# Attention outputs stored in one piece, transfers moved to GpSimd's queue, and a new filling plan in a hybrid decoder block

## The chip, the cores and the metric

The kernel runs on one core of a Trainium2 chip. The metric is the device time of one execution in microseconds (us); the time of a kernel is the median of its runs.

## The reference, cut to what matters

One layer of a decoder: RMSNorm, native sparse attention (three branches with gates), residual, RMSNorm, SwiGLU feed-forward, residual, final RMSNorm. 512 tokens, width 2048, 16 heads of 128 in 4 groups, feed-forward width 5632, all in float32.

```python
h = x
h = h + nsa_mixer(rmsnorm(h, g1), ...)       # DEPTH = 1: layer 0 is the attention mixer
h = h + swiglu(rmsnorm(h, g2), w_in, w_out)
return rmsnorm(h, g3)

# nsa_mixer: proj = h @ w_in gives q, three pairs of k and v, and gates
p_c = masked_softmax(q @ kcc + bias, mask)   # 31 compressed blocks
o_c = p_c @ vcc
...                                          # o_s: selected blocks; o_w: sliding window
o = gates[0] * o_c + gates[1] * o_s + gates[2] * o_w
return o.reshape(S, 2048) @ w_out
```

With 512 tokens there are 8 selectable blocks and up to 16 may be chosen, so the selected branch sees every earlier token, as the window does.

## The kernel before, in words

**Precision.** Each float32 operand is split into a high and a low part (ScalarE, ACT, copies the high part; VectorE, DVE, subtracts). A product is three matmuls (`three`, lines 267 to 269): high x high, low x high, high x low. Weights come as granules of up to 128 x 1024 through the class `Weights`: `load` issues the DMA (line 81) on the queue that `W.queue` names, `split` makes `whi` and `wlo` (lines 97, 98), `take` hands out the next granule and first lets the splits run three granules ahead and the loads three more. There are three raw and four converted buffers.

**The attention stage** (lines 630 to 899) does two kinds of work on TensorE (PE). The first is attention itself, head by head, with the 512 queries in four blocks of 128 (`t`, or `kt` for keys):
- `scores(h, t)`: matmuls into the PSUM tile `s`, DVE adds the bias and takes the maximum (line 791), ACT takes the exponential into `P[t]` (line 793), one part for each branch; the compressed branch goes to `CX[t]`.
- `finish(h, t)`: DVE multiplies by gate over sum (line 805), transposes in blocks of 32 (line 806), and SyncE's queue (SP) stores `P[t]` to memory as `d_p` in four DMAs (line 808).
- `fetch(t)`: SP loads it back, turned, into `PT` (tile `ptr`, line 812).
- `turn(h, b, kt)`: ACT and DVE split a part of `PT` into `pth` and `ptl` (lines 829, 831, 833). `b` is the branch, -1 the compressed one.
- `values(h, b, kt)`: PE multiplies with the values into the PSUM tile `o` (`three`, or line 844 for the compressed branch).
- `head_out(h)`: for heads 0 to 11 the output `o` is split into high and low (`of0`, `of1`; lines 292, 293) and stored in `d_o` (line 855); heads 12 to 15 go straight into `hn_h` and `hn_l`, whose old content is no longer needed by then.

The four `P` are views of two tiles: blocks 0 and 2 share one, 1 and 3 the other.

The second kind of work fills PE in between: `dense()`, a generator that makes the projections of later heads (`qpair`, `kpair`, `vpair`; 32 steps of 650 nominal ns each) and at last four `partial(cb)` (24 steps each), the output projection of heads 0 to 11 for 1024 of the 2048 columns. During the last `qpair` the outputs of heads 0 to 11 come back from memory into `hn_h`, `hn_l` (`reload_o`, line 696). A `partial` loads 512 KB of `x` into the one staging tile (line 702), DVE adds the product (line 717), and the sum goes to `d_h` (line 718).

**Order.** Each engine and each queue works in the order in which its instructions are written out. The program fixes this order by hand: each head has 12 steps, in which the turns, values, fetches of this head stand beside the scores and finishes of the next. After each step `pump(h, step)` draws steps from `dense()` until their nominal sum reaches a goal: 20800 per head up to 13 heads, 18300 after that, always four steps of a head ahead of the position. `drain_to` draws what must be there. Through the stage `W.queue` is GpSimd's queue (POOL); all other DMAs of the stage but one are on SP's.

Of the kernel before, what the change touches and what calls it, by code (L numbers as in the profile page):

```python
# [10 lines left out]
F32 = mybir.dt.float32  # L11
F32R = mybir.dt.float32r
I32 = mybir.dt.int32
AF = mybir.ActivationFunctionType
OP = mybir.AluOpType
# [4 lines left out]
S, D, H, DH, G, HPG = 512, 2048, 16, 128, 4, 4  # L20
NT, KC = S // 128, D // 128
# [152 lines left out]
def nsa_block(ctx: ExitStack, tc: tile.TileContext, x, rel_bias, mix_g, ffn_g, fin_g, w_in, w_out,  # L174
              pos_k, w1k, w2k, pos_v, w1v, w2v, f_in, f_out, onehot, out):
    nc = tc.nc
    mm, act, dve, pool = nc.tensor.matmul, nc.scalar.activation, nc.vector, nc.gpsimd
# [6 lines left out]
    dram = ctx.enter_context(tc.tile_pool(name="dram", bufs=1, space=DRAM))  # L184
# [10 lines left out]
    hn_h, hn_l = hn_t = [hnp.tile([128, KC, S], F32R, name=f"hn_{x}") for x in "hl"]  # L195
    d_t = dram.tile([H, UL], F32, name="d_t")
    d_u = dram.tile([128, H * UL], F32, name="d_u")
    d_c = dram.tile([H, 16 * CL], F32, name="d_c")
    d_o = dram.tile([12, 2, 128, S], F32, name="d_o")
    d_h = dram.tile([S, 256 * N_SPILL], F32, name="d_h")  # L200
    d_r = dram.tile([NT, 128, D], F32, name="d_r")
    d_a = dram.tile([NF // 2, 128, 2 * S], F32, name="d_a")
# [87 lines left out]
    def split_from(psum_ap, hi, lo, scale=None):  # L290
        if scale is None:
            act(hi, psum_ap, AF.Copy)
            dve.tensor_tensor(lo, psum_ap, hi.bitcast(F32), op=OP.subtract)
        else:
            act(hi, psum_ap, AF.Copy, scale=scale)
            dve.scalar_tensor_tensor(lo, psum_ap, scale, hi.bitcast(F32), op0=OP.mult, op1=OP.subtract)
# [53 lines left out]
    with ExitStack() as st1:  # L350
# [11 lines left out]
        with ExitStack() as st0:  # L362
# [79 lines left out]
            p = bank([128, 512])  # L442
            for i in range(N_WARM):
                nc.tensor.transpose(p[:, 128 * (i % 4):128 * (i % 4 + 1)], ident, ident)
            p = bank([128, KC])
# [10 lines left out]
            for q in range(4):  # L456
# [22 lines left out]
                if q == 3:  # L479
                    p = bank([128, S])  # L480
# [100 lines left out]
        for i in range(8):  # L581
# [10 lines left out]
            if i == 1:  # L592
                p = ps1.tile([128, 128], F32, name="tr")
# [27 lines left out]
        p = ps1.tile([96, G, 128], F32, name="tr")  # L621
# [8 lines left out]
    with ExitStack() as st2:  # L630
        ap_ = st2.enter_context(tc.tile_pool(name="ap", bufs=2))
        ps2 = st2.enter_context(tc.tile_pool(name="ps2", bufs=2, space=PSUM))
        kv_tiles(ap_, 1, bufs=1)
        runs = [32 * (2 * t + 3) for t in range(NT)]
        two = [ap_.tile([128, 4 * runs[t]], F32, name=f"p{t}", bufs=1) for t in (2, 3)]
        P = [two[t % 2][:, :4 * runs[t]].rearrange("p (j r) -> p j r", j=4) for t in range(NT)]
        CX = [ap_.tile([128, 32], F32, name=f"cx{t}", bufs=1) for t in range(NT)]
        PT = ap_.tile([128, 4, PT_STEP * 3 + runs[3]], F32, name="ptr", bufs=1)
        d_p = [dram.tile([4, 32, 4, runs[t]], F32, name=f"d_p{t}") for t in range(NT)]
        for t in range(2):  # L640
            pool.memset(two[t], 0.0)
        for t in range(NT):
            pool.memset(CX[t], 0.0)
        done = {"n": 0, "ns": 0}

        def stage_tile():
            return ap_.tile([128, 1024], F32, name="stage", bufs=1)
# [7 lines left out]
        def qpair(h0):  # L655
            ps = proj2()
            end = q_out(ps, h0)
            for i in range(4):
                yield from ws(ps, i, W.take(), end=end)
                if h0 == H - 2 and i < 3:  # L660
                    reload_o(i)
            done["n"] += 1
            yield None

# [27 lines left out]
            yield None  # L692

        def reload_o(i):
            for part, t in enumerate((hn_h, hn_l)):
                nc.sync.dma_start(t[:, 4 * i:4 * i + 4].bitcast(F32),
                                  d_o[4 * i:4 * i + 4, part].rearrange("h p s -> p h s"))

        def partial(cb):
            st = stage_tile().rearrange("p (t c) -> p t c", t=NT)  # L700
            c = slice(256 * cb, 256 * (cb + 1))
            nc.sync.dma_start(st, x[:, c].rearrange("(t p) c -> p t c", p=128))
            ps = [p.rearrange("p (t c) -> p t c", t=2) for p in proj2()]
            for i in range(3):
                w = W.take()
                for t in range(NT):
                    if i == 2 and t == 2:
                        W.ahead(3)
                    for k in range(4):
                        h = 4 * i + k  # L710
                        three(ps[t // 2][:, t % 2], hn_h[:, h, tok(t)], hn_l[:, h, tok(t)], w[0][:, k], w[1][:, k],
                              h == 0 and t % 2 == 0, h == 11)
                        if k % 2:
                            yield 650
                    if i == 2 and t % 2:
                        b = t // 2
                        dve.tensor_tensor(st[:, 2 * b:2 * b + 2], st[:, 2 * b:2 * b + 2], ps[b], op=OP.add)
            nc.sync.dma_start(d_h[:, c].rearrange("(t p) c -> p t c", p=128), st)
            done["n"] += 1
            yield None  # L720

# [12 lines left out]
        STEPS = 12  # L734

        def pump(h, step):
            at = h + (step + 4) / STEPS
            goal = 20800 * min(at, 13) + 18300 * max(at - 13, 0)
            while done["ns"] < goal:
                c = next(stream, "end")  # L740
                if c == "end":
                    return
                done["ns"] += c or 0
# [66 lines left out]
        def fetch(t):  # L810

            nc.sync.dma_start(PT[:, :, PT_STEP * t:PT_STEP * t + runs[t]], d_p[t].rearrange("j a i r -> (j a) i r"))
# [6 lines left out]
        def turn(h, b, kt):  # L819
            n = S - 128 * kt  # L820
            th = ap_.tile([128, 512], F32R, name="pth", bufs=3)
            tl = ap_.tile([128, 512], F32R, name="ptl")
            rows = 128 if b >= 0 else 96
            if b < 0:
                src = arrived(rows, 64, 0, PT_STEP + 64)
            else:
                src = arrived(rows, PT_STEP * kt + 32 * (kt + 1) * b + 32 * kt, kt, PT_STEP + 32 * b)
            th4, tl4 = (x[:rows, :n].rearrange("p (t i s) -> p t i s", i=4, s=32) for x in (th, tl))
            act(th4, src, AF.Copy)
            if b < 0:  # L830
                dve.tensor_tensor(th4[32:64], src[32:64], th4[32:64].bitcast(F32), op=OP.subtract)
            else:
                dve.tensor_tensor(tl4, src, th4.bitcast(F32), op=OP.subtract)
            HS[h]["t", b, kt] = th[:rows, :n], tl[:rows, :n]

        def values(h, b, kt):
            s, g = HS[h], h // HPG
            first = "o" not in s
            if first:
                s["o"] = ps2.tile([128, 512], F32, name="o", bufs=1)  # L840
            th, tl = s.pop(("t", b, kt))
            o = s["o"][:, 128 * kt:]
            if b < 0:
                mm(o, vcc[:, g], th, start=first, stop=True, skip_group_check=True)
            else:
                vh, vl = (v[:, kt, 128 * b:128 * (b + 1)] for v in VV[g % 2])
                three(o, vh, vl, th, tl, first, False)

        def head_out(h):
            o = HS[h]["o"]  # L850
            if h < 12:
                f = [ap_.tile([128, S], F32R, name=f"of{i}", bufs=1) for i in range(2)]
                split_from(o, *f)
                for i in range(2):
                    nc.sync.dma_start(d_o[h, i], f[i].bitcast(F32))
            else:
                split_from(o, hn_h[:, h], hn_l[:, h])
            del HS[h]
# [2 lines left out]
        load_bias(0)  # L861
        load_bias(1)
        for i in range(4):
            scores(0, 3 - i)
            if i:
                finish(0, 4 - i)
            if i > 1:
                fetch(5 - i)
            pump(-1, min(9 + i, 11.7))
        for h in range(H):  # L870
            seq = [(b, kt) for kt in (3, 2, 1, 0) for b in (0, 1)] + [(-1, 0)]
            for i in range(STEPS):
                if i == 4:
                    load_bias(h + 2)
                if i in (0, 3):
                    fetch(1 - i // 3)
                if i < 9:
                    turn(h, *seq[i])
                if i == 8 and h + 1 < H:
                    fetch(3)  # L880
                    fetch(2)
                if i == 0:
                    finish(h, 0)
                if h + 1 < H:
                    if i == 2:
                        drain_to(needed(h + 1))
                    if i % 3 == 2:
                        scores(h + 1, 3 - i // 3)
                    elif i % 3 == 0 and i:
                        finish(h + 1, 4 - i // 3)  # L890
                if 2 <= i < 11:
                    if i == 2 and h % HPG == 0:
                        drain_to(h)
                    values(h, *seq[i - 2])
                    if i == 10:
                        head_out(h)
                pump(h, i)
        W.queue = nc.sync
# [591 lines left out]
```

## Time and profile before

| | |
|---|---|
| median of 3 runs | 2137.48 us (2137.11 to 2138.2) |
| profiled execution | 2137.68 us, its span 2136.0 us |
| PE, weight load, DVE, ACT, POOL busy | 98%, 91%, 77%, 43%, 6% |
| mean granted clock of TensorE | 0.996 |
| read from memory, written | 323.67 MB, 73.50 MB |
| attention stage | about 200 to 710 us of the span |

Busy shares are of the span. A PE that is shown busy need not be at its peak, since matmuls are pipelined and their ends are modelled. An engine that idles off the critical path costs nothing by that. In lists of waits the columns are: engine and tile that waited, line, what ended the wait, then microseconds in total, number of times, and the longest.

### The profile page before, as it was taken

Reading aid. Unit: us, or ns where it says so; the run is one execution under the profiler, and the core shown is the slowest. Engines: PE = TensorE matmul, PEld = TensorE weight load, DVE = VectorE, ACT = ScalarE, POOL = GpSimd, SP = SyncE. Lnnn points to the kernel's source line nnn. Section 1 sums busy time; section 2 is a strip of 40 time slices with the busy share of each in tenths; the row PEclk is TensorE's granted clock in tenths of the full one; section 3 lists DMA queues with packets and bytes.
Section 4 is the critical chain, followed back from the end, with each engine's and each line's share of the span. In section 5 each row is a group of like instructions: output and inputs, shape, how many; then the busy total and the mean of one; then the engine's idle time right before and its main releaser. Section 6 shows DMA issues by size and latency. Waiting matters only on the chain.

```text
span 2136.0 us, 37198 instructions
## 1 busy us (share of the span) xinstructions
PE 2103.2 (98%) x14697; PEld 1949.5 (91%) x14697; DVE 1634.8 (77%) x2680; ACT 922.9 (43%) x1433; POOL 118.2 (6%) x195
## 2 busy tenths in 40 slices
PE   9999999999998999999999999999999999999998
PEld 7898788898988889899999999999999888999996
DVE  5565777878776357898888888888888787877785
ACT  5344454555544234444444343443434444544344
POOL 1000111111100000000000000000000000001000
PEclk9999999999999999999999999999999999999999
DMA  7555777776787643344434344433344776878894
GB/s 226 174 158 149 195 203 202 194 209 197 207 295 211 218 137 111 118 130 128 129 126 122 122 126 129 129 119 125 123 129 129 256 278 220 299 268 308 307 336 143
DMA packets 279147, 394.37 MB, mean 185 GB/s; under 512 B 34763, under 2 KB 208891, under 8 KB 278332
## 3 DMA queue, kind: packets, MB, share of 16 engines
q1 hardware_dynamic: 255324, 289.68, 43.5%
q0 software_dynamic: 21744, 98.12, 13.3%
q10 hardware_dynamic: 1904, 4.20, 0.5%
q8 instruction: 115, 1.88, 0.4%
q14 instruction: 60, 0.49, 0.1%
HBM read 323.67 MB, written 73.50 MB: 186 GB/s over the span
## 4 chain that ended last, share of the span: by engine, by line
PE 87%; DVE 5%; DMA 4%; ACT 2%; issue 2%; SPq 1%; POOL 0%; ACTq 0%; DVEq 0%; POOLq 0%
PE f L268 19%; PE f L269 19%; PE f L267 19%; PE proj L267 7%; PE proj L268 6%; PE proj L269 6%; DMA d_p<-p 1%; DVE wlo L98 1%; DMA ptr<-d_p 1%; PE pp L269 1%; PE pp L268 1%; PE pp L267 1%; PE po L269 1%; PE po L267 1%; PE po L268 1%
## 5 line engine op out<-in xcount | busy, mean ns | idle before, releaser
L98 DVE TENSOR_TENSOR wlo<-raw,whi 128x1024 fp32r<-128x1024 f32 (+1 forms) x226 | 270.6, 1200 | 117.2 <-ACT whi L97 116.7
L97 ACT ACTIVATE whi<-raw 128x1024 fp32r<-128x1024 f32 (+1 forms) x226 | 234.4, 1040 | 230.4 <-DVE raw L989 124.7
L989 DVE TENSOR_TENSOR tlo<-tt,thi 128x1536 fp32r<-128x1536 f32 (+2 forms) x135 | 197.1, 1460 | 110.1 <-ACT thi L1091 89.1
L267 PE MATMUL f<-hn_h,whi 128*128 128x256 f32 x984 | 271.7, 276 | 0.8 <-ACT E L1049 0.8
L269 PE MATMUL f<-hn_h,wlo 128*128 128x256 f32 x984 | 271.6, 276 | 0.0
L268 PE MATMUL f<-hn_l,whi 128*128 128x256 f32 x984 | 271.6, 276 | 0.0
L1086 ACT ACTIVATE whi<-raw 128x1024 fp32r<-128x1024 f32 x123 | 126.1, 1057 | 292.2 <-DVE raw L989 281.9
L267 PE MATMUL proj<-hn_h,whi 128*128 128x512 f32 x512 | 204.1, 399 | 0.5 <-ACT hn_h L402 0.5
L268 PE MATMUL proj<-hn_l,whi 128*128 128x512 f32 x512 | 200.7, 392 | 0.3 <-DVE hn_l L403 0.3
L269 PE MATMUL proj<-hn_h,wlo 128*128 128x512 f32 x512 | 200.9, 392 | 0.0
L267 PEld LDWEIGHTS f<-hn_h,whi 128*128 128x128 f32 x984 | 184.7, 188 | 1.2 <-ACT E L1049 1.2
L269 PEld LDWEIGHTS f<-hn_h,wlo 128*128 128x128 f32 x984 | 184.7, 188 | 0.0
L268 PEld LDWEIGHTS f<-hn_l,whi 128*128 128x128 f32 x984 | 184.7, 188 | 0.0
L1091 ACT ACTIVATE thi<-tt 128x1536 fp32r<-128x1536 f32 x82 | 121.8, 1486 | 84.8 <-PE f L268 75.3
L989 DVE TENSOR_TENSOR wlo<-raw,whi 128x1024 fp32r<-128x1024 f32 x123 | 147.0, 1223 | 0.0
L267 PE MATMUL proj<-whi,hn_h 128*128 128x256 f32 (+2 forms) x496 | 146.7, 296 | 0.0
L269 PE MATMUL proj<-whi,hn_l 128*128 128x256 f32 (+2 forms) x496 | 146.0, 294 | 0.0
L268 PE MATMUL proj<-wlo,hn_h 128*128 128x256 f32 (+2 forms) x496 | 145.9, 294 | 0.0
L269 PE MATMUL f<-whi,tlo 128*128 128x512 f32 x320 | 124.9, 390 | 0.6 <-DVE tlo L989 0.6
L268 PE MATMUL f<-wlo,thi 128*128 128x512 f32 x320 | 125.0, 391 | 0.0
L267 PE MATMUL f<-whi,thi 128*128 128x512 f32 x320 | 124.7, 390 | 0.0
L269 PEld LDWEIGHTS proj<-hn_h,wlo 128*128 128x128 f32 x512 | 96.5, 189 | 21.5 <-DVE wlo L98 0.2
(323 smaller groups left out, 6087.1 us busy)
## 6 DMA issues: line engine op xcount, KB each, us to landing
raw<-in_ffn_w_in SPq DMA_DIRECT2D x135, 512.0 KB, 3.8
raw<-in_ffn_w_out SPq DMA_DIRECT2D x88, 512.0 KB, 5.7
rawx<-in_ffn_w_in SPq DMA_DIRECT2D x41, 512.0 KB, 4.8
rawx<-d_a SPq DMA_DIRECT2D x31, 512.0 KB, 5.2
ah<-d_s POOLq DMA_DIRECT2D x16, 896.0 KB, 7.0
al<-d_s POOLq DMA_DIRECT2D x16, 896.0 KB, 9.5
raw<-in_nsa_w_in SPq DMA_DIRECT2D x24, 512.0 KB, 5.1
raw<-in_nsa_w_in POOLq DMA_DIRECT2D x24, 512.0 KB, 4.7
```

Source lines behind the costliest of these rows:

```text
L97: self.nc.scalar.activation(hi[:, :n], src, AF.Copy)
L98: self.nc.vector.tensor_tensor(lo[:, :n], src, hi[:, :n].bitcast(F32), op=OP.subtract)
L267: mm(o, ah, bh, start=start, stop=False, skip_group_check=True)
L268: mm(o, ah, bl, start=False, stop=False, skip_group_check=True)
L269: mm(o, al, bh, start=False, stop=stop, skip_group_check=True)
L989: dve.tensor_tensor(o, a, b, op=OP.subtract)
L1086: act(h, r, AF.Copy)
L1091: act(h, ttf, AF.Copy)
```

## The change

- `d_o` becomes three arrays of four heads in float32. `head_out` copies `o` once (ACT) into the staging tile and stores that, 12 stores of 256 KB instead of 24.
- `reload_o(i)` loads four heads in one DMA into `hn_l`, on GpSimd's queue instead of SP's; a new `split_o(k)` then splits two heads in place. It stands twice in the last `qpair` and four times in the first `partial`.
- A `partial`'s load of `x` and store of `d_h` go to GpSimd's queue; the load is written out at the second granule instead of at the start.
- Each of the four `P` has a tile of its own, all set to zero, block 3 first. `of0` and `of1` are gone. The compressed branch takes no `ptl` tile.
- `pump`: the lead over the position is 4 + max(5 - 2 x position, 0) steps, 11 at one head before the first, 4 from position 2.5 on. After 13 heads the goal grows by 22500 per head instead of 18300. Ahead of head 0, filling is drawn before each block of scores instead of after, and a fetch is issued ahead of the finish of its turn of the loop.
- `values` of the compressed branch and `head_out` move from step 10 to step 11.

```diff
-    d_o = dram.tile([12, 2, 128, S], F32, name="d_o")
+    d_o = [dram.tile([4, 128, S], F32, name=f"d_o{i}") for i in range(3)]
...
-        two = [ap_.tile([128, 4 * runs[t]], F32, name=f"p{t}", bufs=1) for t in (2, 3)]
-        P = [two[t % 2][:, :4 * runs[t]].rearrange("p (j r) -> p j r", j=4) for t in range(NT)]
+        P = [ap_.tile([128, 4, runs[t]], F32, name=f"p{t}", bufs=1) for t in range(NT)]
...
-        for t in range(2):
-            pool.memset(two[t], 0.0)
-        for t in range(NT):
+        for t in reversed(range(NT)):
             pool.memset(CX[t], 0.0)
+            pool.memset(P[t], 0.0)
...
                 if h0 == H - 2 and i < 3:
                     reload_o(i)
+                if h0 == H - 2 and i > 1:
+                    split_o(i - 2)
...
         def reload_o(i):
-            for part, t in enumerate((hn_h, hn_l)):
-                nc.sync.dma_start(t[:, 4 * i:4 * i + 4].bitcast(F32),
-                                  d_o[4 * i:4 * i + 4, part].rearrange("h p s -> p h s"))
+            pool.dma_start(hn_l[:, 4 * i:4 * i + 4].bitcast(F32), d_o[i].rearrange("h p s -> p h s"))
+
+        def split_o(k):
+            h, l = (x[:, 2 * k:2 * k + 2] for x in (hn_h, hn_l))
+            act(h, l.bitcast(F32), AF.Copy)
+            dve.tensor_tensor(l, l.bitcast(F32), h.bitcast(F32), op=OP.subtract)
 
         def partial(cb):
...
-            nc.sync.dma_start(st, x[:, c].rearrange("(t p) c -> p t c", p=128))
             ps = [p.rearrange("p (t c) -> p t c", t=2) for p in proj2()]
             for i in range(3):
                 w = W.take()
+                if i == 1:
+                    pool.dma_start(st, x[:, c].rearrange("(t p) c -> p t c", p=128))
                 for t in range(NT):
+                    if not cb and i < 2 and t % 2 == 0:
+                        split_o(2 + 2 * i + t // 2)
...
-            nc.sync.dma_start(d_h[:, c].rearrange("(t p) c -> p t c", p=128), st)
+            pool.dma_start(d_h[:, c].rearrange("(t p) c -> p t c", p=128), st)
...
         def pump(h, step):
-            at = h + (step + 4) / STEPS
-            goal = 20800 * min(at, 13) + 18300 * max(at - 13, 0)
+            at = h + step / STEPS
+            at += (4 + max(5 - 2 * at, 0)) / STEPS
+            goal = 20800 * min(at, 13) + 22500 * max(at - 13, 0)
...
-            tl = ap_.tile([128, 512], F32R, name="ptl")
+            tl = ap_.tile([128, 512], F32R, name="ptl") if b >= 0 else th
...
             if h < 12:
-                f = [ap_.tile([128, S], F32R, name=f"of{i}", bufs=1) for i in range(2)]
-                split_from(o, *f)
-                for i in range(2):
-                    nc.sync.dma_start(d_o[h, i], f[i].bitcast(F32))
+                f = stage_tile()[:, :S]
+                act(f, o, AF.Copy)
+                nc.sync.dma_start(d_o[h // 4][h % 4], f)
...
         for i in range(4):
+            pump(-1, 4.5 + 2 * i)
             scores(0, 3 - i)
+            if i > 1:
+                fetch(5 - i)
             if i:
                 finish(0, 4 - i)
-            if i > 1:
-                fetch(5 - i)
-            pump(-1, min(9 + i, 11.7))
+        pump(-1, 11.7)
...
-                if 2 <= i < 11:
+                if 2 <= i < 10 or i == 11:
...
-                    values(h, *seq[i - 2])
-                    if i == 10:
+                    values(h, *seq[min(i - 2, 8)])
+                    if i == 11:
                         head_out(h)
                 pump(h, i)
```

## The prediction

> **What bounds the kernel now.** First the page: the matrix engine's share, and the chain of work that ended last.
>
> ```profile
> span 2136.0 us, 37198 instructions
> PE 2103.2 (98%) x14697; PEld 1949.5 (91%) x14697; DVE 1634.8 (77%) x2680; ACT 922.9 (43%) x1433; POOL 118.2 (6%) x195
> PE 87%; DVE 5%; DMA 4%; ACT 2%; issue 2%; SPq 1%; POOL 0%; ACTq 0%; DVEq 0%; POOLq 0%
> ```
>
> PE is busy 98% of the time, and the change takes no matmul away, so it can only win back PE's idle time. All edits lie in the attention stage (about 200 to 710 us). Next view: the stage in three stretches (the second number is PE's busy time; after POOL's come the granted clock, the DMA engines' busy share and GB/s).
>
> ```profile
> 240.00:600.00 360.00, 358.21 (x2027) 313.31 (x2026) 284.61 (x787) 183.46 (x491) 50.78 (x68) 1.00 0.72 206
> 600.00:710.00 110.00, 100.41 (x740) 94.90 (x739) 72.11 (x186) 44.78 (x111) 9.55 (x13) 0.97 0.71 226
> 200.00:240.00 40.00, 33.23 (x152) 26.62 (x151) 28.08 (x86) 18.09 (x50) 3.00 (x4) 0.96 0.61 166
> ```
>
> Idle: 6.77 us at the start, 1.79 in the long middle, 9.59 at the end. The granted clock, 1.00 in the middle, is 0.96 of the 40 us at the start and 0.97 of the 110 at the end, where PE idles most: 1.6 and 3.3 us more. So there is 8.4 + 1.8 + 12.9 = 23.1 us to win. It may be somewhat more, since ends of matmuls are modelled:
>
> ```profile
> 201.51 0.39 PE L269 MATMUL proj<-hn_h,wlo 128*128 128x512 f32 x1
> 203.62 0.37 PE L267 MATMUL s<-k0h,qh 128*128 128x288 f32 x1 [1.72 <-DVE yt L319]
> ...
> 205.30 0.23 PE proj L267
> ```
>
> At the chain's pace of 0.23 us the next matmul could have started at 201.74, so this gap is 1.88 us and not the 1.72 shown. Twenty such waits would add some 3 us.
>
> Who is waited for: PE at the start (two rows), in the middle (one), at the end (three); then the ACT wait of the whole stage that an own place for P touches; then SP's queue at the end.
>
> ```profile
> PE o L267 <- issue: 2.5, 1, 2.5
> PE o L268 <- DVE ptl L833: 1.8, 1, 1.8
> ...
> PE o L844 <- DVE pth L831: 1.3, 4, 0.4
> ...
> PE o L267 <- ACT pth L829: 5.6, 3, 2.7
> PE o L268 <- DVE ptl L833: 2.3, 1, 2.3
> PE o L844 <- DVE pth L831: 1.3, 1, 1.3
> ...
> ACT p L793 <- DMA d_p<-p: 4.1, 2, 3.6
> ...
> SPq L812 <- DMA d_p<-p: 28.8, 15, 5.2
> SPq L702 <- DMA d_h<-stage: 10.1, 3, 4.4
> SPq L718 <- DVE stage L717: 3.5, 2, 2.4
> ```
>
> PE always waits for turned probabilities (pth, ptl), that is for the round trip scores, exponential, normalising, d_p, ptr, turn. What makes that trip late differs from place to place.
>
> **The start (8.4 us).** Filling is counted in steps of 650 nominal, three 512-column matmuls: 3 x 0.23 = 0.69 us. Before, 10 steps stand ahead of head 0, and none ahead of its first scores. The new formula gives 8 ahead of the first scores (goal 4767) and 24 ahead of head 0 (goal 15167), 14 x 0.69 = 9.7 us more PE work at the place where PE starves. The 8 steps (5.5 us) cover the 1.9 us gap before the first scores and push the trip back by 3.6 us; the other idle time (4.9) and the slow clock (1.6) stand against the rest of the 9.7. The trip itself shortens: scores 1 and 0 no longer wait until the stores of P[3] and P[2] are read (the 4.1 us of ACT above), and the fetch of block 3 is issued before finish(0, 2). The four memsets grow from 2048 to 3072 columns on GpSimd, about 1 us, hidden under the 5.5 us of filling. I take 7.5 of 8.4; bounds 5 and 8.4.
>
> **Heads 0 to 2, which pay for it.** Steps emitted up to the end of head 2 are 104 either way, so heads 0, 1, 2 hold 25, 27, 28 steps where a full head holds 32.
>
> ```profile
> 246.48 0.40 PE L844 MATMUL o<-pth,vcc 96*128 96x512 f32 x1
> 276.40 0.50 PE L844 MATMUL o<-pth,vcc 96*128 96x512 f32 x1
> ...
> 240.00:270.00 30.00, 30.00 (x148) 25.38 (x147) 23.98 (x67) 15.13 (x40) 3.00 (x4) 1.00 0.71 202
> L293 DVE TENSOR_TENSOR of<-o,of x12: 652/653/692, 251.0 to 582.4; 128x512 fp32r<-128x512 f32 x12
> L98 DVE TENSOR_TENSOR wlo<-raw,whi 128x1024 fp32r<-128x1024 f32 (+1 forms) x226 | 270.6, 1200 | 117.2 <-ACT whi L97 116.7
> ```
>
> The last matmul of a head's values (L844) marks heads: 29.9 us for a full head. With 7 steps less, head 0 has 29.9 - 4.8 = 25.1 us of PE work; heads 1 and 2 have 26.5 and 27.2. DVE was busy 24.0 of 30 us; less one L293 (the output is no longer split) and 7/8 of one weight split (8 steps use one), it needs 24.0 - 0.65 - 1.05 = 22.3. It fits, but with 2.8 us to spare in which its waits must fit too. Bounds: 0, or what two heads of such length lose further down (9.4). I take 1.5, nearer to 0, because the lost heads have causes of their own.
>
> **The middle (1.8 us).** values(-1) moves from step 10 to step 11, behind one more pump (2.7 steps, 1.8 us) and the next head's scores. The longest such wait is 0.4 us, so all go. Next late would be head_out, which now follows at step 11 and only copies; the next head's first values are three steps off. Turn 8's buffer is held one step longer, and of three buffers the next is wanted at step 2 of the next head: no new wait. I take 1.6.
>
> **The end (12.9 us).**
>
> ```profile
> 608.79 0.50 PE L844 MATMUL o<-pth,vcc 96*128 96x512 f32 x1 [1.33 <-DVE pth L831]
> 641.24 0.40 PE L844 MATMUL o<-pth,vcc 96*128 96x512 f32 x1
> 672.69 0.40 PE L844 MATMUL o<-pth,vcc 96*128 96x512 f32 x1
> ...
> 608.77 10.80 DMA ptr<-d_p
> 683.49 6.22 DMA ptr<-d_p
> ...
> ptr<-d_p SPq DMA_DIRECT2D x16, 192.0 KB, 2.9
> hn_h<-d_o SPq DMA_DIRECT2D x3, 1024.0 KB, 8.7
> hn_l<-d_o SPq DMA_DIRECT2D x3, 1024.0 KB, 10.1
> ah<-d_s POOLq DMA_DIRECT2D x16, 896.0 KB, 7.0
> d_h<-stage SPq DMA_DIRECT2D x4, 512.0 KB, 3.7
> ```
>
> Heads 13 and 14 take 32.5 and 31.5 us though they hold only 18300 / 650 = 28.2 steps, worth 29.9 - 2.7 = 27.2: 5.3 and 4.3 us are lost. Three causes, and what the change does to each:
> - The fetch at 608.77 takes 10.80 us, because six loads of 1 MB come back around it. Three stay, each behind its own granule's matmuls on GpSimd's queue, 8 steps of 32 or some 7.5 us apart; by the nearest row (896 KB, 7.0 us) one has landed when the next starts. The 2.9 us behind this fetch mostly go.
> - SP stands 10.1 us before the three loads of x that need the staging tile back, and 3.5 before the stores; whatever d_p stores and fetches are queued behind stand too. On GpSimd's queue the same waits hold up weight loads, and those are asked for six granules ahead, over 30 us.
> - Scores 1 no longer wait for P[3], so a late store does not delay the next scores.
>
> Filling also rises to 22500 a head, 34.6 steps: heads 13 and 14 get 29.9 + 1.8 = 31.7 us of work, as long as they last now. The price is at the very end: when head 15 starts, 62400 - 2.33 x 22500 = 9900 nominal of the partials is left (15 steps, 10.5 us; now 30 steps), and after step 5 nothing covers it. The trip there ran from 672.69 to the last fetch, asked for at about 690 and landing 2.9 us later (median): 20.8 us, of which SP's hold made up to 4.4. The cover is 10.5 us and 3 us of values; with the hold gone 2.9 us stay open, less as the other stores come sooner. I leave 1.9 at this place and nothing for the rest: gain 11.0, bounds 6 and 12.9.
>
> **Elsewhere, at nothing.** Six new splits of the returned outputs (two slices of 512 columns, as large as a weight split: 1.04 us ACT, 1.20 DVE each) stand in heads 12 and 13, where 31.7 us of filling cover them; uncovered they cost 7 us, and ACT would stand if a return is late: it is read two granules after its issue, some 15 us, against 7.0. Twelve L293 go. The d_o stores halve; they stay on SP.
>
> **Sum.** 7.5 - 1.5 + 1.6 + 11.0 = 18.6 us. The profiled execution took 2137.68 us (1.68 beside its span), 0.2 above the median: 2137.7 - 18.6 = 2119 us.
>
> **A rule on GpSimd's queue.** Three returns, four loads and four stores move to it.
>
> ```profile
> raw<-in_nsa_w_in SPq DMA_DIRECT2D x24, 512.0 KB, 5.1
> raw<-in_nsa_w_in POOLq DMA_DIRECT2D x24, 512.0 KB, 4.7
> ```
>
> The same 512 KB load lands in 4.7 us from this queue and in 5.1 from SP's, with DVE busy beside it. So I charge the queue nothing. The Trainium skill, page "SBUF — State Buffer", section "Who interferes with whom", says the contrary can hold: a DMA issued from GpSimd needs GpSimd to write its descriptors, and VectorE in a two-port mode locks it out meanwhile. Its example grows from 620 to 3100 ns; an estimate by that page is eleven times 2.5, 27 us of this queue's time, and if PE waited for all of it the sum would be 8 us slower, 2146. The two rows speak against it: this queue's load is the quicker one. Its chance, 0.03, stands within that of rival 3 below.
>
> **The rivals.**
> 1. *The filling taken from heads 0 to 2 was needed.* DVE and ACT wait on one another (ACT for scores, DVE for pth), and a 25 us head is shorter than their loop. For it: heads 13 and 14, with 27.2 us of work, took over 31. Against it: SP's holds and the returns explain those. Price: 9.4 us instead of 1.5, so 18.6 - 7.9 = 10.7 gained: 2127.
> 2. *It is traffic, not order.* The late fetches are slow because weights, x, d_h and P share the DMA engines, whoever issues them (the last number of the rows below: 397 GB/s at 600, against 206 in the long middle). The end then gains 2 us instead of 11: 18.6 - 9 = 9.6, 2128. Against: half of the returned bytes go, 10.1 us of SP's wait are order, and from 640 on the rate is back at 229. The Trainium skill, page "DMA: Bandwidth & Descriptors", section "Issuing engines are not separate DMA queues", is on this side: another issuing engine saves only the sequencer's time. The 10.1 us of SP's waits speak against it, since the rule does not count what stands queued behind a wait.
>
> ```profile
> 600.00:610.00 10.00, 8.67 (x53) 7.45 (x52) 8.87 (x20) 4.28 (x10) 1.50 (x2) 1.00 1.05 397
> ...
> 640.00:650.00 10.00, 9.62 (x79) 9.24 (x78) 5.63 (x21) 4.05 (x14) 0.75 (x1) 1.00 0.77 229
> ```
>
> 3. *Slower: weights arrive late behind the new waits on GpSimd's queue.* Place: the four partials. The queue stands for PE's last matmul, then 3.7 us for the store of d_h, then a weight load (5.4 us, in the row below) and its split (1.04 + 1.20) follow: 11.3 us. It decides when fewer than two converted granules (8 steps, 5.5 us each) are left; with one, 5.8 us and 1.6 of slow clock are lost four times, 29.6. Gains of 18.6 stand against it: 11 us slower, 2149. For it: this queue does wait in order. Against: three converted granules are kept, 16.5 us.
>
> ```profile
> raw<-in_nsa_w_out POOLq DMA_DIRECT2D x17, 512.0 KB, 5.4
> L97 ACT ACTIVATE whi<-raw 128x1024 fp32r<-128x1024 f32 (+1 forms) x226 | 234.4, 1040 | 230.4 <-DVE raw L989 124.7
> ```
>
> **How the numbers follow.** Forecast 0.55, its own range 2111 to 2126 (the bounds of start, heads 0 to 2 and end not all at once, and 3 us for the modelled ends). Rival 1: 0.23. Rival 2: 0.11. Rival 3: 0.11. The range 2109 to 2131 takes in rivals 1 and 2; outside it lie rival 3 and some hundredths on either side. A difference of 0.2% is 4.3 us, about what can be told from no change, so faster means under 2133.2: the forecast and rivals 1 and 2 alone, 0.83; within 0.2%, 0.06 out of rivals 1 and 2: both together leave 18.6 - 7.9 - 9 = 1.7 us, 2136; slower 0.11, rival 3.
>
> **What would show it.** Right: in 200 to 240 PE idle below 2 us and the clock at 1.00; no L844 wait from 240 to 600; no wait of SP for d_h, the slowest fetch of the end under 8 us, PE idle from 600 to the stage's end below 3. The marks of heads 13 and 14 should lie 31 to 32 us apart, now full of work, and the stage should end near 692 instead of 710. Wrong: waits for pth or ptl in heads 0 to 2 (rival 1), fetches of 10 us without a wait of SP (rival 2), ACT or PE waiting for raw or whi in the partials (rival 3).

## The result, and the profile after

The changed kernel takes 2157.25 us (median of 4 runs, 2151.36 to 2157.66) against 2137.84 us: ratio 1.0086, 95% interval 1.0073 to 1.0099. It is slower by 19 us where 18.6 us less were forecast. Its profiled execution took 2157.43 us.

First the page after: PE's share is unchanged, the span is 19.7 us longer.

```profile
span 2155.7 us, 37155 instructions
PE 2114.1 (98%) x14697; PEld 1954.4 (91%) x14697; DVE 1636.0 (76%) x2674; ACT 929.5 (43%) x1439; POOL 128.2 (6%) x209
```

Then the attention stage in stretches; columns as in the prediction (length, PE busy, weight loads, DVE, ACT, POOL, granted clock, DMA share, GB/s). The granted clock is the share of its full speed that TensorE was given.

```profile
200.00:225.00 25.00, 25.00 (x119) 20.73 (x118) 17.02 (x49) 10.46 (x29) 4.69 (x10) 1.00 0.48 131
225.00:320.00 95.00, 84.83 (x398) 68.45 (x397) 67.03 (x182) 42.46 (x113) 10.67 (x14) 0.95 0.61 170
320.00:600.00 280.00, 279.96 (x1630) 246.81 (x1629) 217.00 (x614) 143.94 (x389) 41.04 (x55) 1.00 0.69 199
600.00:640.00 40.00, 26.56 (x127) 22.09 (x126) 23.51 (x54) 15.44 (x35) 2.99 (x4) 0.79 0.61 191
640.00:710.00 70.00, 69.57 (x562) 68.16 (x561) 54.68 (x144) 33.35 (x85) 11.85 (x16) 1.00 0.67 202
710.00:731.00 21.00, 19.21 (x105) 15.65 (x105) 8.81 (x12) 7.23 (x11) 2.94 (x4) 0.84 0.65 207
```

Idle time and lost clock added up, 200 to 225 and the long middle lose nothing any more, and 640 to 710 loses 0.4 us. But 225 to 320 (heads 0 to 2) loses 10.2 + 4.8 = 15.0 us, 600 to 640 (head 12) 13.4 + 8.4 = 21.8, and the stage's last stretch 1.8 + 3.4 = 5.2. That makes 42.4 us where the kernel before lost 23.1: 19.3 of the 19.7 us are here.

Who PE waits for, in 225 to 320 (three rows) and in 600 to 640 (four), and what ACT waits for there:

```profile
PE o L268 <- DVE ptl L840: 4.7, 8, 0.9
PE o L267 <- ACT pth L836: 3.4, 2, 2.3
PE o L267 <- issue: 1.6, 1, 1.6
...
PE proj L267 <- ACT hn_h L699: 5.3, 1, 5.3
PE o L268 <- DVE ptl L840: 3.3, 3, 2.9
PE proj L269 <- DVE hn_l L700: 2.4, 1, 2.4
PE o L267 <- ACT pth L836: 2.4, 2, 1.8
...
ACT pth L836 <- DMA ptr<-d_p: 10.6, 2, 5.4
```

L699 and L700 are the new splits of the returned outputs. The marks of the heads (last matmul of a head's values, now L851) show the same in whole heads: head 1 takes 33.6 us, head 12 takes 49.3 (31.3 before), heads 13 and 14 take 32.9 and 31.5.

```profile
256.44 0.40 PE L851 MATMUL o<-pth,vcc 96*128 96x512 f32 x1
290.04 0.40 PE L851 MATMUL o<-pth,vcc 96*128 96x512 f32 x1
...
588.54 0.40 PE L851 MATMUL o<-pth,vcc 96*128 96x512 f32 x1
637.79 0.40 PE L851 MATMUL o<-pth,vcc 96*128 96x512 f32 x1
670.68 0.40 PE L851 MATMUL o<-pth,vcc 96*128 96x512 f32 x1
702.18 0.40 PE L851 MATMUL o<-pth,vcc 96*128 96x512 f32 x1
```

Cut at these marks, the loss of 225 to 320 has two parts. The first row is the kernel before, from 200 to the mark of its head 0; the other two are the changed kernel, up to the mark of head 0 and from there to that of head 1.

```profile
200.00:246.50 46.50, 39.73 (x184) 32.07 (x183) 33.57 (x95) 20.27 (x54) 4.50 (x6) 0.96 0.61 165
...
225.00:256.44 31.44, 26.97 (x112) 21.09 (x111) 21.06 (x54) 12.83 (x32) 1.50 (x2) 0.89 0.61 170
256.44:290.04 33.60, 28.80 (x129) 22.66 (x128) 25.41 (x72) 15.57 (x42) 4.48 (x6) 0.95 0.65 186
```

Up to the mark of head 0 the kernel before loses 8.6 us and the changed one 7.9: the loss of the start is still there, only later. Head 1 loses another 6.5, head 2 0.9 (the clock in these rows is rounded).

### The profile page after: what moved, and what is told of

The parts are those of the page before. It is cut to its first block, busy times and chain, and to the rows that moved or that the text cites. A ratio compares the mean times of both kernels' runs of the same rounds, so it can differ in the third digit from the quotient of the medians.

```text
span 2155.7 us, 37155 instructions
## 1 busy us (share of the span) xinstructions
PE 2114.1 (98%) x14697; PEld 1954.4 (91%) x14697; DVE 1636.0 (76%) x2674; ACT 929.5 (43%) x1439; POOL 128.2 (6%) x209
## 4 chain that ended last, share of the span: by engine, by line
PE 64%; DMA 2%; DVE 2%; ACT 1%; issue 0%; SPq 0%; ACTq 0%; DVEq 0%
PE f L268 19%; PE f L269 19%; PE f L267 19%; PE pp L267 1%; PE pp L268 1%; PE pp L269 1%; PE proj L267 1%; PE proj L268 1%; PE proj L269 1%; PE po L268 1%; PE po L267 1%; PE po L269 1%; DMA d_p<-p 1%; DMA ptr<-d_p 1%; DMA tt<-d_a 0%
```

## The experiments

Medians stand beside that of the kernel before on the same chip; ratios are to it, with 95% intervals. Differences are read between runs that stand beside the same median of the kernel before, unless the text says otherwise.

**Parts of the changed kernel undone (kernel before 2136.08 us).** A lead of 4 everywhere:

```diff
-            at += (4 + max(5 - 2 * at, 0)) / STEPS
+            at += 4 / STEPS
```

> The changed kernel with one part undone: the lead of the filling is 4 steps of a head everywhere again (goal 22500 after 13 heads kept). Theory A (the lead is paid back out of heads 0 to 2, which then hold 25, 27 and 28 steps and starve): in the changed kernel the stretch 225 to 320 loses 10.2 us of PE idle time and 4.8 of slow clock, the start nothing; here heads 0 to 2 lose under 2 and the start loses again 6 to 8, so about 2157 - 14 + 7 = 2150. Rival (the stretch 225 to 320 starves for another reason: own places for P, step 11, the order ahead of head 0): it keeps its 15 us and the start comes on top, about 2164.

Measured 2142.08 us, 1.0033 (1.0023 to 1.0044). Three stretches of its profile:

```profile
200.00:240.00 40.00, 32.63 (x147) 25.84 (x146) 26.74 (x85) 18.19 (x50) 3.23 (x5) 0.96 0.60 166
240.00:320.00 80.00, 80.00 (x444) 69.85 (x443) 62.72 (x174) 39.68 (x109) 11.20 (x15) 1.00 0.68 191
575.00:640.00 65.00, 53.04 (x295) 46.53 (x294) 43.24 (x113) 31.20 (x76) 7.51 (x11) 0.87 0.63 198
```

Heads 0 to 2 lose nothing after 240, the start loses its 9 us, head 12 keeps its loss (47.9 us). It was better by 8 us than theory A said: the lead costs more than it wins, by far. What it wins is the difference between these 9.0 us and the 7.9 that the changed kernel loses up to the mark of head 0.

The same lead paid back slowly:

```diff
-            at += (4 + max(5 - 2 * at, 0)) / STEPS
+            at += (4 + 5 * max(12 - at, 0) / 12) / STEPS
```

> The changed kernel, but the lead falls slowly: 4 + 5 x (12 - position) / 12 steps, so about 9 steps ahead of head 0 and 4 from head 12 on; the payback is 0.4 steps of a head for each of twelve heads instead of 5 in two and a half. Theory A: the start keeps its gain and heads 0 to 2 lose 1 to 3 us instead of 15: about 2144. Rival (it is the lead itself, the chain of head 0 pushed back behind 24 steps, that starves heads 0 to 2): the stretch 225 to 320 keeps over 10 us of its loss, about 2155.

Measured 2169.07 us, 1.0149 (1.0134 to 1.0164). Theory A failed. The rival's stretch came as it said: 225 to 320 loses 11.3 us (PE idle 6.6, clock 0.95), 10.5 of them before the mark of head 0 (at 258.1). Its time did not: the run is worse than the changed kernel, though each head gives up little over one step of filling. By their marks heads 3, 6 and 10 take 35.0, 33.7 and 34.3 us, their neighbours 29 to 31. One step less can't be the reason there; the next idea was the position of the filling against the 12 steps (the run with a fixed lead of 7.5, below).

Without the six splits, and in a second run without the returns (the call of `reload_o`) too. Both leave old content where the returned outputs belong, so the partials multiply other numbers; only the times are read from them.

```diff
-                if h0 == H - 2 and i > 1:
-                    split_o(i - 2)
...
-                    if not cb and i < 2 and t % 2 == 0:
-                        split_o(2 + 2 * i + t // 2)
```

> The changed kernel without the six splits of the returned outputs (left out: hn_h keeps old content for heads 0 to 11); the three returns of 1 MB stay. In the changed kernel 600 to 640 loses 13.4 us of idle PE and 8.4 of slow clock. Theory B (the returns' traffic makes the fetches of P land late, 7.8 us each, and the splits only queue behind that): only the waits named for the splits go, 5.3 + 2.4 us and their part of the slow clock, about 2147. Rival C (the splits themselves, 2.2 us each on ACT and DVE at the tightest place, make the stall): nearly all of it goes, about 2138.

> As the run without the splits, and the three returns of 1 MB are left out too (the partials multiply old content). Theory B: the fetches at 598 and 607 land in 4 to 6 us instead of 7.8, 600 to 640 loses under 4 us, about 2138, some 9 us below the run without splits alone. Rival C: no more than 2 us below that run.

Measured 2143.81 us, 1.0034 (1.0023 to 1.0045), and 2133.7 us, 0.999 (0.998 to 1.0). Head 12 goes from 49.3 to 37.6 us without the splits and to 29.8 without the returns as well. So both theories hold in part: in this order of leaving out, 11.7 us are the splits', 7.8 the returns'. The fetches of block 1 (320 KB) in 580 to 640, first with the returns and then without:

```profile
ptr<-d_p SPq DMA_DIRECT2D x2, 320.0 KB, 5.4
...
ptr<-d_p SPq DMA_DIRECT2D x2, 320.0 KB, 3.2
```

These are medians of two fetches, of which the first alone meets the returns: it takes 7.6 us with them and 3.2 without.

**Which queue, and one piece or two (lead 4; kernel before 2137.22 us).** Returns on SP's queue:

```diff
-            pool.dma_start(hn_l[:, 4 * i:4 * i + 4].bitcast(F32), d_o[i].rearrange("h p s -> p h s"))
+            nc.sync.dma_start(hn_l[:, 4 * i:4 * i + 4].bitcast(F32), d_o[i].rearrange("h p s -> p h s"))
```

> The kernel with the lead of 4 everywhere (2142 us; head 12 takes 47.9 us from mark to mark, 29.8 without returns and splits), and the three returns of 1 MB issued on SP's queue instead of GpSimd's. Theory Q (it is the queue: on GpSimd's the returns run beside the fetches of blocks 1 and 0, which then land in 8 us instead of 3; on SP's they stand in order behind them): head 12 falls to 38 to 42, about 2134. Theory S (the splits at the head of the first partial cost the 11 us whatever the returns do): head 12 above 44, about 2140 or more.

Measured 2135.93 us, 1.0002 (0.9993 to 1.0012). That is 1.3 us under its own kernel before, where the run with the returns on GpSimd's queue (2142.08) was 6.0 above its own; by the two ratios the queue costs 6.6 us. Head 12 takes 42.1 us instead of 47.9. Returns and fetches of block 1 in 570 to 640, on GpSimd's queue and on SP's:

```profile
hn_l<-d_o POOLq DMA_DIRECT2D x3, 1024.0 KB, 8.1
ptr<-d_p SPq DMA_DIRECT2D x2, 320.0 KB, 6.1
```

```profile
hn_l<-d_o SPq DMA_DIRECT2D x3, 1024.0 KB, 7.8
ptr<-d_p SPq DMA_DIRECT2D x2, 320.0 KB, 3.4
...
PE proj L267 <- ACT hn_h L699: 5.9, 1, 5.9
PE proj L269 <- DVE hn_l L700: 2.1, 1, 2.1
```

On SP's queue the fetch stands ahead of the return and lands in 3.4 us (theory Q; the first of the two fetches alone takes 3.5 us instead of 8.9). The wait for the splits stays, 8.0 us (theory S). The two add.

Two pieces as before the change, through the two halves of the staging tile, with the returns on SP's queue and then on GpSimd's (here cut to `head_out`; `d_o` and `reload_o` take both pieces again, the later splits go, and the lead is 4):

```diff
-                f = stage_tile()[:, :S]
-                act(f, o, AF.Copy)
-                nc.sync.dma_start(d_o[h // 4][h % 4], f)
+                st = stage_tile()
+                f = [st[:, S * i:S * (i + 1)].bitcast(F32R) for i in range(2)]
+                split_from(o, *f)
+                for i in range(2):
+                    nc.sync.dma_start(d_o[h // 4][i, h % 4], st[:, S * i:S * (i + 1)])
```

> Lead of 4 everywhere, and the outputs as before the change: split at head_out into high and low (both in the staging tile, 24 stores), six returns of 1 MB on SP's queue, no later splits; own places for P, x and d_h on GpSimd's queue, step 11 and the goal of 22500 stay. If the one-piece outputs with their late splits are what went wrong (Q and S together): head 12 back to about 31 us as in the kernel before, 2142 - 16 = 2126, 10 us faster than the kernel before. If the bytes that come back count most (6 MB instead of 3): head 12 at 38 or more, 2134 or more.

> As the run with two pieces on SP's queue, but the six returns of 1 MB on GpSimd's queue. Theory Q: twice the bytes beside the fetches of blocks 1 and 0, head 12 at 38 to 45, so 2134 to 2140 and 8 us or more above the run on SP's queue. Theory S (only the splits cost): within 3 us of that run, about 2127.

Measured 2135.6 us, 0.9989 (0.9979 to 0.9999), and 2141.8 us, 1.0027 (1.0014 to 1.0039). Head 12 takes 32.2 and 43.3 us. On SP's queue the six returns leave head 12 within 1 us of the kernel before, which has them there too; the queue alone costs 6.2 us, less than the 8 or more of theory Q, though head 12 is where it said. The 2126 that was expected did not come: the middle heads take 30.3 us (29.9 with one piece) and heads 13 to 15 lose again, by marks 93.0 us in place of 84.5 in the run with one piece on SP's queue. The profiled execution of the run on SP's queue lies 5 us above its median, so the last figure may be too high.

The lead fixed at 7.5, every full head with 32 steps:

```diff
-            at += (4 + max(5 - 2 * at, 0)) / STEPS
+            at += 7.5 / STEPS
```

> The changed kernel with a lead of 7.5 steps everywhere, neither falling nor 4; every full head holds 32 steps again. It tells why heads 0 to 2 of the changed kernel and heads 3, 6 and 10 of the slowly falling lead lose 4 to 5 us. Theory P (position: the ends of the projections, with their copies and subtractions on ACT and DVE, meet the turns at other steps of a head, whatever the filling): several of the heads 0 to 11 take 33 to 35 us at this lead though none is thin, 2160 or more. Rival T (thin heads alone): heads 0 to 11 stay at 30.0 and only head 12 and the start differ, 2140 to 2145.

Measured 2169.02 us, 1.0151 (1.0136 to 1.0166). Theory P holds, with a smaller loss in every head instead of a large one in some: marks of heads 2 and 3, then what DVE waits for at a weight split in 330 to 560, here and in the kernel before.

```profile
318.08 0.40 PE L851 MATMUL o<-pth,vcc 96*128 96x512 f32 x1
350.34 0.40 PE L851 MATMUL o<-pth,vcc 96*128 96x512 f32 x1
...
DVE wlo L98 <- ACT whi L97: 45.5, 29, 2.3
```

```profile
DVE wlo L98 <- ACT whi L97: 2.5, 8, 0.5
```

A head takes 32 us, 2 more, with the same instructions. At this position the ACT half of a weight split is queued behind the exponentials (L800), and DVE, in order, stands 45.5 us instead of 2.5 before it. One such place, on ACT and on DVE:

```profile
379.66 0.50 ACT L800 ACTIVATE p<-u,mx 128x256 f32<-128x256 f32 x1
...
380.15 1.04 ACT L97 ACTIVATE whi<-raw 128x1024 fp32r<-128x1024 f32 x1
...
381.23 1.23 DVE L98 TENSOR_TENSOR wlo<-raw,whi 128x1024 fp32r<-128x1024 f32 x1 [1.77 <-ACT whi L97]
```

The same wait stands in 225 to 320 of the changed kernel, first row, and hardly in the kernel before:

```profile
DVE wlo L98 <- ACT whi L97: 10.2, 7, 2.3
...
DVE wlo L98 <- ACT whi L97: 0.8, 3, 0.3
```

But position at this lead is not all of it. By marks, heads 1 and 2 of the changed kernel take 62.9 us for work that the prediction put at 26.5 + 27.2 = 53.7, so 9.2 are lost (7.4 by idle time and clock; the ends of matmuls are modelled). With a lead of 7.5 and full heads they take 63.5 for twice 29.9, so 3.7.

**Goals (two pieces on SP's queue, lead 4; kernel before 2136.0 us), and two parts alone.**

```diff
-            goal = 20800 * min(at, 13) + 22500 * max(at - 13, 0)
+            goal = 20800 * min(at, 13) + 18300 * max(at - 13, 0)
```

> The run with lead 4 and two-piece outputs on SP's queue (2135.6 us), with the goal after 13 heads back at 18300 instead of 22500. So against the kernel before it keeps own places for P, step 11, x and d_h on GpSimd's queue and the order ahead of head 0. Theory E (22500 empties the filling by step 5 of head 15 and leaves its round trip open: that run loses 6 us of gaps and 2.9 of slow clock from 690 to its end): the end is covered again, heads 13 and 14 take 28 to 30 us, about 2129. Rival (the late heads are short of something else than filling): heads 13 and 14 still over 31, about 2135.

> As the run with 18300, with 20000. Theory E: 24 steps are left for head 15 instead of 15; within 2 us of the run with 18300, below the one with 22500 by 4 or more: about 2130. Rival: no difference among the three goals.

Measured 2137.54 us, 1.0009 (0.9999 to 1.0018), and 2133.13 us, 0.9985 (0.9976 to 0.9995). Theory E was wrong for 18300: less filling did not make the end better. 20000 is 4 us better than 18300, so the rival is wrong too. Against 22500 it wins little: it is 2.9 us under its kernel before, where 22500 was 1.6 under its own.

Into the kernel before, x and d_h on GpSimd's queue alone, and step 11 alone (both as in the diff of the change):

> The kernel before, with one part of the change alone: a partial's load of x and store of d_h on GpSimd's queue, x at the second granule. As predicted (SP's 10.1 us of standing before x is what makes the fetches of heads 14 and 15 late): SP no longer waits for d_h, marks of heads 13 and 14 at 28 to 29 us instead of 32.4 and 31.4, about 2131. Rival (the traffic of returns and weights makes them late): 2135 to 2138, the marks as before.

> The kernel before, with the compressed branch's values and head_out at step 11 instead of 10, nothing else. As predicted: heads 1 to 10 at 29.8 instead of 30.1 us, no wait at the marks, 1.6 to 3 us less, about 2135. Rival (the later head_out holds the output's PSUM place and the next head waits): no gain or up to 3 us more.

Measured 2135.3 us, 0.9993 (0.9984 to 1.0003), and 2139.61 us, 1.0018 (1.0008 to 1.0027). For x and d_h the time is the rival's. SP no longer waits before x, and head 14 shortens (31.4 to 29.1), but head 13 hardly does (32.4 to 32.2), and head 15 gives it back (28.6 to 31.0, in a profiled execution 2.9 us above the median). Step 11 alone takes the waits at the marks away and still makes the heads 0.3 us longer: DVE now stands for the output's copy, a wait that the kernel before does not list in 300 to 560.

```profile
DVE of L293 <- ACT of L292: 12.0, 9, 1.5
```

**Each suspected part alone in the kernel before (2135.72 us).** The edits are those of the change: the lead's line; the outputs in one piece with returns on GpSimd's queue and splits; x and d_h with a goal of 20000; the same with own places for `P`.

> The kernel before (2136 to 2137 us) with the falling lead alone (4 + max(5 - 2 x position, 0) steps in the filling's goal; order ahead of head 0, places, queues, goal 18300 as before). Theory P (the position of the filling against the steps costs, whatever the rest): heads 0 to 2 lose 8 to 15 us, the waits of DVE for the ACT half of a weight split grow there, the start gains up to 7: 2140 to 2146. Rival (it costs only with the order and places of the changed kernel): heads 0 to 2 at 26 to 28 us, the start better, 2130 to 2134.

> The kernel before with the outputs alone changed: one float32 piece by way of the staging tile, three returns on GpSimd's queue, six later splits. Theory (returns beside the fetches and splits in front of the first partial cost by themselves): head 12 from 31.3 to 42 to 49 us, heads 1 to 10 0.2 us shorter each, 2136 + 14 - 2 = 2148, from 2142 to 2152. Rival (the loss needs the fuller late heads): 2134 to 2138.

> The kernel before with x and d_h on GpSimd's queue and the goal after 13 heads at 20000. If SP's standing and too little filling in heads 13 and 14 are what was to be won at the end: 2131 to 2133, 3 to 5 us under the kernel before. If head 15 needs what the others get: 2135 to 2138.

> As the run with x and d_h moved and goal 20000, with own places for the four P besides (the two output pieces lie in the staging tile instead). If own places shorten the trip at the start and at the end as predicted (ACT's 4.1 us of waits for d_p): 2 to 4 us less than that run, 2128 to 2131. Rival (other waits end last there): the same within 1.5 us.

Measured: lead 2151.99 us, 1.0076 (1.0061 to 1.0091); outputs 2149.25 us, 1.0071 (1.0055 to 1.0087); x, d_h and 20000 2128.58 us, 0.9973 (0.9962 to 0.9983); with own places 2128.49 us, 0.9963 (0.995 to 0.9976). The stretch 225 to 320 of the lead alone, the waits of PE in 580 to 640 of the outputs alone, and the end of the third:

```profile
225.00:320.00 95.00, 83.11 (x369) 65.91 (x370) 68.30 (x192) 40.84 (x114) 9.93 (x13) 0.95 0.63 176
```

```profile
PE proj L267 <- ACT hn_h L701: 4.9, 1, 4.9
PE proj L269 <- DVE hn_l L702: 2.1, 1, 2.1
```

```profile
600.00:704.00 104.00, 99.28 (x752) 93.66 (x751) 71.95 (x186) 44.93 (x111) 16.29 (x22) 1.00 0.78 248
```

Both losses stand by themselves: 16.3 and 13.5 us. The lead's is larger than either theory said; 200 to 320 loses 19.4 us there (2.8 up to 225, 16.6 behind it), 11 more than in the kernel before, and DVE's wait for the ACT half of a weight split grows as theory P said (9.8 us). The time of the outputs alone is what its theory said. With x, d_h and 20000 the end loses 4.7 us instead of 12.9, and the time is below the 2131 to 2133 expected. Own places change nothing that can be measured.

Last, the goal alone, and x and d_h with the change's own goal (kernel before 2135.76 us):

```diff
-            goal = 20800 * min(at, 13) + 18300 * max(at - 13, 0)
+            goal = 20800 * min(at, 13) + 20000 * max(at - 13, 0)
```

> The kernel before with the goal after 13 heads at 20000 instead of 18300, nothing else. If the filling is what heads 13 and 14 lacked and SP's standing is covered by it: about 2129, as with x and d_h moved. If both are needed (SP stands 10 us before x and the trip of head 15 stays late): 2134 to 2137.

> The kernel before with x and d_h on GpSimd's queue and the change's goal of 22500. If the filling is then used up too early in head 15, as the gaps from 690 on in the run with two-piece outputs said: 2 to 5 us above the run with 20000 (2128.6), 2131 to 2134. As predicted for the end (the cover is long enough but for 1.9 us): 2127 to 2129.

Measured 2137.34 us, 1.001 (1.0001 to 1.0019), and 2129.18 us, 0.997 (0.9957 to 0.9982). With x still on SP's queue the filling alone gains nothing, and SP's wait is still there:

```profile
SPq L702 <- DMA d_h<-stage: 10.5, 3, 4.1
```

So it takes both, the move of x and d_h and more filling, and then 22500 is as good as 20000. These versions, 7 us under the kernel before, beat both kernels.

## Why the prediction was wrong

**The start.** "I take 7.5 of 8.4" failed. Filling ahead of head 0 did not remove the loss of the start; it moved it. 200 to 225 loses nothing, but up to the mark of head 0 the changed kernel loses 7.9 us where the kernel before loses 8.6, and with a lead of 4 it is 9.0. So under 1 us was won. The sign that was named, PE idle below 2 us and a clock of 1.00 in 200 to 240, was missed as well: 3.7 us and 0.96. PE still waits for the first turned probabilities. Why the trip of head 0 did not get shorter was not tried.

**Heads 0 to 2.** "I take 1.5" failed too: by marks heads 1 and 2 lose 9.2 us, and the lead alone costs 16.3 us net. That is the place and the price (9.4) of rival 1, but its mechanism, thin heads, is not shown. The sum treated filling as interchangeable, so many steps of 0.69 us wherever they stand. With 32 steps to a unit and to a head, a lead of 4 puts the splits and ends of projections at the same steps of every head, and a lead of 7.5 costs 2 us in every head with the same work. A falling lead carries the first heads through other positions, and with the slow fall heads 3, 6 and 10 take 4 to 5 us more than a full head though they are only one step short. How much of the 9.2 us is position and how much thinness was not separated.

**The end, returns.** "The 2.9 us behind this fetch mostly go" failed. Half of the bytes came back, but beside the fetches of blocks 1 and 0, which took 8.0 and 7.8 us: 7.8 us of head 12. In the kernel before, the fetch of block 1 stood ahead of the returns in one queue and took 3.4 us, that of block 0 stood between them and took 6.0. The order of one queue had protected the first; rival 2 priced the traffic and missed that. Moving only the queue is worth 6 us (6.6 by ratio with one piece, 2141.8 against 2135.6 with two). The Trainium skill, page "DMA: Bandwidth & Descriptors", section "Issuing engines are not separate DMA queues", has all queues interleave on the same engines and another issuer save only issue time. The interleaving is what these runs show; the 6 us come from what no longer stands ahead.

**"Elsewhere, at nothing".** The six splits were hidden under 31.7 us of filling in the sum. But four of them stand in the first partial, ahead of the very matmuls that are that filling: PE waited 5.3 + 2.4 us for L699 and L700, and the splits make 11.7 us of head 12. The uncovered price that was given, 7 us, was nearer, and left out the slow clock.

**The end, order and filling.** "SP stands 10.1 us before the three loads of x" was right, and so was the filling, as a pair. The term of 11.0 us measured 6.6 (the run with 22500) without the outputs in one piece. "I leave 1.9 at this place" for head 15 was 5.2 in the changed kernel.

**The middle.** Right in the changed kernel (29.9 us a head instead of 30.1, and 320 to 600 loses nothing), but only with the output no longer split at step 11: with two pieces at step 11 the heads take 30.3, and in the kernel before the step alone costs 3.6 us. The sum did not name this condition.

**Own places** were given a part in the start and the end; in the kernel with x, d_h and 20000 they are worth 0.1 us, within noise. The new order ahead of head 0 was not tried alone. **Rival 3** did not appear: no wait of PE that the profile lists in the two lost stretches is for a weight.

**The sum of the parts.** 16.3 + 13.5 - 6.6 = 23.2 us stands beside the 19.4 measured; step 11 with one-piece outputs explains some 2 of the difference (0.2 us in ten heads), the rest stays open.

## What to carry to other kernels

Where two streams of work are interleaved by hand, moving one against the other is not free even when every step is kept: compare the period at the new position before counting what the move fills. Work put ahead of a wait may only push the wait back: read what was lost up to a fixed piece of work, not up to a fixed time. A transfer that waits its turn in one queue may be protecting the transfer ahead of it; before it goes to another queue, look at which transfers it will then meet. Work that feeds the cover can't be hidden by that cover.

## What the runs showed of the hardware that was not expected

In 620 to 630 of the changed kernel, where PE stood 5.3 us in one piece, the clock was 0.62, and it stayed at 0.70 in the next slice although PE was busy 7.61 of 10 us:

```profile
620.00:630.00 10.00, 2.84 (x10) 2.16 (x10) 7.86 (x20) 5.88 (x13) 1.50 (x2) 0.62 0.62 194
630.00:640.00 10.00, 7.61 (x49) 7.57 (x50) 5.26 (x13) 2.78 (x10) 0.00 (x0) 0.70 0.46 127
```

The waits of 600 to 640 thus cost 8.4 us of clock beside 13.4 of idle time. The Trainium skill, page "TensorE: Matmul & The Clock Gate", section "Part 1: The HAM clock gate (the "warmup" mystery)", has the clock at half after an idle window of about 3.4 us and back after a busy one. The half agrees: in slices of 1 and 2 us the clock is 0.50 from 623 to 636, and it is back 3.6 us after PE is busy again (632.4). The idle window does not: near 240 the clock fell to half behind two waits of 1.13 and 0.90 us, with a matmul between them.

```profile
238.72 0.39 PE L267 MATMUL o<-pth,v0h 128*128 128x256 f32 x1 [1.13 <-ACT pth L836]
240.01 0.52 PE L268 MATMUL o<-ptl,v0h 128*128 128x256 f32 x1 [0.90 <-DVE ptl L840]
...
239.00:240.00 1.00, 0.11 (x1) 0.00 (x0) 1.00 (x3) 0.52 (x1) 0.07 (x1) 1.00 0.11 29
241.00:242.00 1.00, 1.00 (x4) 0.81 (x3) 0.97 (x3) 0.00 (x0) 0.00 (x0) 0.50 0.75 165
```

The load of x lands in 7.2 us (median of four) from GpSimd's queue, where it took 3.8 from SP's (last row, the kernel before; one of those four took 7.1), while weight loads of the same size on GpSimd's queue take 4.6:

```profile
raw<-in_nsa_w_out POOLq DMA_DIRECT2D x18, 512.0 KB, 4.6
stage<-in_x POOLq DMA_DIRECT2D x4, 512.0 KB, 7.2
...
stage<-in_x SPq DMA_DIRECT2D x4, 512.0 KB, 3.8
```

It was late for its use once: DVE waited 1.3 us for it, PE did not. Why it is slower was not tried.
